# Finer tile pools around attention, and longer assumed landings in the planner, in a hybrid attention and retention block

## The chip, the cores and the metric

The kernel runs on one core of one Trainium2 chip. The metric is the device time of one execution in microseconds (us). The core has TensorE (PE, matmuls; its weight loads are PEld), VectorE (DVE), ScalarE (ACT), GpSimd (POOL) and SyncE (SP), which issues most of the transfers; POOL issues the others. On-chip memory is SBUF; matmuls write into PSUM banks.

## The reference

One layer on x of 1024 positions by 1024 channels, in float32. The input is normalized and projected once; the columns are split over attention (queries, keys and values), retention and gates.

```python
h = rms_norm(x, norm1_g[l])
z = jnp.einsum('bsd,dn->bsn', h, w_in[l])
zq, zkv, zg, zr, zm = jnp.split(z, splits, axis=-1)
y_nsa = nsa_attention(...)   # compressed + selected + sliding-window branches
y_ret = retention(...)       # 4 heads, chunks of 128, group norm, silu gate
u = jnp.einsum('nbsc,ncd->bsnd', jnp.stack([y_nsa, y_ret]), w_branch[l])
gates = jax.nn.sigmoid(zm.reshape(b, s, N_BRANCH, D_MODEL))
mixed = jnp.sum(gates * u, axis=2)
x = x + jnp.einsum('bsd,de->bse', mixed, w_out[l])
h = rms_norm(x, norm2_g[l])
x = x + (jax.nn.silu(h @ ffn_w_gate[l]) * (h @ ffn_w_up[l])) @ ffn_w_down[l]
```

The attention has 8 heads in 2 groups of keys and values. Its first branch attends to 63 compressed keys (a small network over blocks of 32 positions), its second to the 8 blocks of 64 positions that the first one's weights select, its third to the last 512 positions. The feed-forward width is 2816.

## The kernel before, in words

**Arithmetic.** Each float32 operand is split into a high and a low part, and a product is three matmuls (high by high, high by low, low by high). The retention projections use sums of quarters of the normalized input: the tiles gS1 to gS4 hold such sums, the tiles op those of the weights. Each psS, psF, psO, psT names a ring of PSUM banks.

**The order.** The program is not written in the order in which it runs. Each piece of work is a generator that yields operations (`Op`) with a cost, an added latency and the tiles that they read and write. The class `Sched` holds the generators as streams, models the time at which each engine is free and each tile is ready, and always takes the operation with the earliest modelled start; a stream's priority and lateness break near ties. For a transfer it models the issue, the bytes over 360 per ns, and 1000 ns; the `lat` of the operation is added before the tile counts as ready. So a change of an assumed time changes the order on every engine behind it. On the chip, each engine runs its instructions in the order thus written, and a waiting instruction holds those behind it on its engine or queue.

**The tiles.** SBUF is divided in pools that are opened and closed like a stack. A new tile at an address that an earlier, closed pool has covered waits for the last uses of each pool that lies under its own pool. The pools that matter: `gpr` (gS2, gS3 and three buffers gt) on the right side, and `gpl` (gS1, gS4, op, xx, Ta, Tb and three buffers ga) on the left hold the retention projections; both are closed together by `gps.close()`. Behind them `kvp` (kT and vv, keys and values of a group), `ap` (P, pT, comb, cim, cv, cgt and others of the softmax) and `tb` (Mt, Ltri, Fb, which are mask tables; two buffers qt for queries; one buffer zs for gates) are opened on the same addresses.

**The stages,** by the starts in the trace: norm and first projections; the compression (`compress`, L636, run twice, for keys and for values) amid the projections of queries, 60 to 130 us; the retention projections to about 375 us; attention with retention and the gates of the merge as filler, to about 805 us; then `branch1` and `merge_main`, which multiply the two branches by their weights, the output projection and the feed-forward.

**The places that the change and the prediction touch.** In `compress` the gathered input is loaded into the tile cX in two halves, TensorE transposes it 128 columns at a time (L318, psT), VectorE adds the position terms, and TensorE multiplies with cw into psO. The filler beside it is the projection, `whA,H`, and transposes of queries (qcat), whose results SyncE stores to q_scr. `load_group` (L1499) issues kT and vv from POOL, `q_loads` (L827) the qt, also from POOL, and `tables2` builds the mask tables on POOL. The first scores of attention are the matmuls `kc,qt` (compressed keys), then `kT,qt`. The retention projections store their results to r_scr through gt and ga (SP). `merge_gates` multiplies the gates of the merge (`H,wh`), ScalarE writes them to zs, and SP stores them to z_scr. After attention, `y_loads` and `y_split` bring the branch outputs back (yraw) and write them to H. `mx_loads` (L1596) loads what branch1 stored to u_scr, and `merge_out` (L1602) loads the gates again (sgm), combines them with the matmuls' result on VectorE and adds to mx.

The step by which the planner counts a transfer and its latency:

```python
self.bus = max(self.bus, end + 650) + r.bytes / 360.0
end = self.bus + 1000
...
self.ready[k] = max(self.ready.get(k, 0.0), end + r.lat)
```

Of the kernel before, what the change touches and what calls it, by code (L numbers as in the profile page):

```python
# [9 lines left out]
F32 = mybir.dt.float32  # L10
F32R = mybir.dt.float32r
# [5 lines left out]
T = 1024  # L17
# [4 lines left out]
HD = 64  # L22
# [18 lines left out]
def nel(ap):  # L41
    n = 1
    for d in ap.shape[1:]:
        n *= d
    return n
# [212 lines left out]
def kernel(  # L258
# [20 lines left out]
    pe, act, dve, gp, sp = nc.tensor, nc.scalar, nc.vector, nc.gpsimd, nc.sync  # L279
# [26 lines left out]
    def sb_ring(pool, shape, dt, name, bufs):  # L306
        return Ring([lambda: pool.tile(shape, dt, name=name, bufs=bufs)] * bufs)
# [56 lines left out]
    def dma(o, i, eng=None):  # L364
        n = nel(o) * 4 * o.shape[0]
        r = Op("gp", 1040, 0, [o], [i], lambda: gp.dma_start(o, i)) if eng is gp else \  # L366
            Op("sp", 50, 0, [o], [i], lambda: sp.dma_start(o, i))
        r.bytes = n
        return r
# [33 lines left out]
    k_scr = [dram.tile([128, 2, T], F32, name=f"k_scr{br}") for br in range(2)]  # L403
    v_scr = [dram.tile([128, 2, NT, 128], F32, name=f"v_scr{br}") for br in range(2)]
# [50 lines left out]
    rings = {"wo": None}  # L455
# [16 lines left out]
    kT, vv = [[], []], [[], []]  # L472
# [163 lines left out]
    def compress(kv, pc):  # L636
# [8 lines left out]
        for g in range(2):  # L645
            base = c_scr[kv, g]
            yield dma(X[g * 64:(g + 1) * 64, :],
                      bass.AP(tensor=base.tensor, offset=base.offset, ap=[[16 * HD, 64], [1, 2048]]))
# [176 lines left out]
    qt, qref = {}, {}  # L825
# [24 lines left out]
    gps = ExitStack()  # L850
    gpr = gps.enter_context(tc.tile_pool(name="gpr", bufs=1, side="right"))
    gm, gops, gT1, gT2, gT4, gt = {}, {}, {}, {}, {}, {}
    for j in (2, 3):
        gm["S", j] = gpr.tile([128, 2, 4, 512], F32R, name=f"gS{j}")
    gt_ring = Bag([gpr.tile([128, 512], F32, name=f"gt{n}") for n in range(3)])
# [363 lines left out]
    gpl = gps.enter_context(tc.tile_pool(name="gpl", bufs=1))  # L1219
    for j in (1, 4):  # L1220
        gm["S", j] = gpl.tile([128, 2, 4, 512], F32R, name=f"gS{j}")
    gm["Ta"], gm["Tb"] = [sb_ring(gpl, [128, 4, 128], F32, n, 2) for n in ("Ta", "Tb")]
    gm["op"] = [gpl.tile([128, 2, 8, 128], F32R, name="op", bufs=2) for _ in range(2)]
    gt_ring.tiles.extend(gpl.tile([128, 512], F32, name=f"ga{n}") for n in range(3))
    gm["aw"] = gt_ring
    gm["xx"] = gpl.tile([128, 2048], F32, name="xx")
# [5 lines left out]
    es = ExitStack()  # L1232
    kvp = es.enter_context(tc.tile_pool(name="kvp", bufs=1))
    ap_ = es.enter_context(tc.tile_pool(name="ap", bufs=2))
    tb = es.enter_context(tc.tile_pool(name="tb", bufs=1))
    rqs = ExitStack()
    rp = rqs.enter_context(tc.tile_pool(name="rp", bufs=1, side="right"))
    rings["q"] = sb_ring(tb, [128, 2, 4, 128], F32R, "qt", 2)
# [28 lines left out]
    zs_ring = sb_ring(tb, [128, 512], F32, "zs", 1)  # L1267
# [28 lines left out]
    cb_ring = sb_ring(ap_, [128, T], F32, "comb", 1)  # L1296
    comb, pcT, Pt, Ob = {}, {}, {}, {}
# [50 lines left out]
    def select(u, pn):  # L1348
        g, i = u
        yield Wait(lambda: "lt" in fl and "st" in fl)  # L1350
        im = ap_.tile([128, 3, 64], F32, name="cim", bufs=1)
# [4 lines left out]
        v = ap_.tile([128, 4, 16], F32, name="cv", bufs=1)  # L1356
# [7 lines left out]
        gt = ap_.tile([128, 2, 16, 16], F32, name="cgt", bufs=1)  # L1364
# [134 lines left out]
    def load_group(g):  # L1499
        yield Wait(lambda: us[0] in qt)  # L1500
        for br in (1, 0):
            kT[br].append(kvp.tile([128, T], F32R, name=f"kT{br}"))
            vv[br].append(kvp.tile([128, NT, 128], F32R, name=f"vv{br}"))
            yield dma(kT[br][g], k_scr[br][:, g], gp)
            yield dma(vv[br][g], v_scr[br][:, g], gp)
            fl.add("kv1")
        fl.add(("gkv", g))
# [123 lines left out]
    es = ExitStack()  # L1631
# [693 lines left out]
```

## Time and profile before

| | |
|---|---|
| three runs, us | 1597.06, 1598.1, 1599.48 (median 1598.1) |
| profiled execution, us | 1598.91 |
| its span, us | 1597.2 |
| mean granted TensorE clock | 0.993 |
| TensorE busy | 1558.2 us, 98%, 8299 matmuls |
| VectorE busy | 1034.4 us, 65% |
| ScalarE busy | 742.4 us, 46% |
| GpSimd busy | 294.2 us, 18% |

All times of the trace are microseconds from the start of the span. A line of the timeline groups neighbouring instructions of one line and form: start, time that they take together, engine, line, operation, written and read tiles, and a count; in brackets is the idle time of the engine ahead of them, with what ended it. SPq is SyncE's issue of a transfer; its landing is another time, which the view of a tile gives as a minimum, median and maximum. Matmuls are pipelined, so that the last one's end reaches over the next one's start. The granted clock is that of TensorE as a share of full speed.

### The profile page before, as it was taken

The numbers are of one execution on the slowest core, as the hardware profiler recorded it, in microseconds if no ns is written. First come the engines' busy times: TensorE is split into PE (matmuls) and PEld (weight loads), VectorE is DVE, ScalarE is ACT, GpSimd is POOL, SyncE is SP. The second block draws the span as 40 slices with busy tenths as digits, with TensorE's granted clock in tenths as the row PEclk, the third lists the DMA queues.
The fourth block names the chain that finished last, engine by engine and source line by source line (L and its number), as shares of the span: only waits on it lengthen the run. The fifth ranks groups of instructions, "written<-read, shape, count | busy, mean of one in ns | idle before, by whom it ended". The sixth has DMA issues, their size and how long they took to land.

```text
span 1597.2 us, 23177 instructions
## 1 busy us (share of the span) xinstructions
PE 1558.2 (98%) x8299; PEld 1339.0 (84%) x8299; DVE 1034.4 (65%) x2163; ACT 742.4 (46%) x1512; POOL 294.2 (18%) x387
## 2 busy tenths in 40 slices
PE   8989999998999999999999999999999999999999
PEld 8989888887989898897887887888888888788887
DVE  7346655543798967789839449656666555477674
ACT  6234343333777667677524326333333333344442
POOL 4233100002132211221000101332343332000000
PEclk9999999999999999999999999999999999999999
DMA  5565364326333245225476322534344544397521
GB/s 179 159 170 159 111 183 119 118 86 192 99 100 119 81 139 165 73 78 179 140 257 211 132 80 80 184 132 142 135 134 150 178 141 141 120 403 256 180 78 53
DMA packets 191573, 233.06 MB, mean 146 GB/s; under 512 B 21857, under 2 KB 123233, under 8 KB 191202
## 3 DMA queue, kind: packets, MB, share of 16 engines
q1 hardware_dynamic: 178978, 193.84, 37.5%
q0 software_dynamic: 12480, 37.75, 7.1%
q8 instruction: 65, 1.06, 0.3%
q14 instruction: 50, 0.41, 0.1%
HBM read 159.18 MB, written 72.37 MB: 145 GB/s over the span
## 4 chain that ended last, share of the span: by engine, by line
PE 81%; DVE 5%; DMA 3%; ACT 1%; issue 1%; POOL 0%; SPq 0%; DVEq 0%; ACTq 0%
PE psS L313 27%; PE psF L313 26%; PE psO L313 12%; PE psT L313 11%; PE psT L318 4%; DMA qt<-q_scr 1%; DVE P L1302 1%; DMA mx<-u_scr 1%; DVE pT L343 1%; PE psF L318 0%; DVE H L343 0%; DVE wh L343 0%; DMA sg<-z_scr 0%; DVE P L348 0%; DVE T L343 0%
## 5 line engine op out<-in xcount | busy, mean ns | idle before, releaser
L313 PE MATMUL psF<-H,wh 128*128 128x512 f32 x780 | 200.2, 394 | 4.7 <-DVE H L343 2.8
L313 PE MATMUL psS<-H,wh 128*128 128x512 f32 x684 | 187.2, 404 | 3.9 <-DVE sgm L353 3.1
L313 PEld LDWEIGHTS psF<-H,wh 128*128 128x128 f32 x780 | 142.9, 188 | 31.0 <-DVE H L343 3.3
L313 PEld LDWEIGHTS psS<-H,wh 128*128 128x128 f32 x684 | 126.5, 192 | 25.7 <-issue 3.5
L333 ACT ACTIVATE P<-P,pm 128x640 f32<-128x640 f32 (+7 forms) x128 | 94.1, 735 | 45.8 <-DVE pm L1302 43.4
L343 DVE TENSOR_TENSOR pT<-psT,pT 128x512 fp32r<-128x512 f32 (+1 forms) x152 | 92.1, 615 | 32.9 <-ACT pT L333 32.6
L313 PE MATMUL psS<-kT,qt 128*128 128x384 f32 (+3 forms) x384 | 102.9, 346 | 1.0 <-ACT zs L333 0.9
L333 ACT ACTIVATE pT<-psT 128x512 fp32r<-128x512 f32 (+1 forms) x152 | 77.7, 533 | 42.9 <-PE psT L318 42.5
L313 PE MATMUL psO<-pT,vv 128*128 128x256 f32 x528 | 91.3, 290 | 1.8 <-DVE pT L343 1.7
L313 PE MATMUL psS<-whA,H 128*128 128x256 f32 (+1 forms) x672 | 89.9, 288 | 0.0
L313 PEld LDWEIGHTS psO<-pT,vv 128*128 128x128 f32 x528 | 79.2, 189 | 11.2 <-DVE pT L343 4.1
L313 PEld LDWEIGHTS psS<-whA,H 128*128 128x128 f32 x672 | 83.6, 189 | 0.0
L318 PE MATMUL psT<-ident,P 128*128 128x128 f32 x528 | 77.2, 273 | 0.2 <-DVE pT L343 0.2
L313 PEld LDWEIGHTS psS<-kT,qt 128*128 128x128 f32 x384 | 65.7, 192 | 8.1 <-ACT zs L333 1.1
L343 DVE TENSOR_TENSOR wh<-wraw,wh 128x512 fp32r<-128x512 f32 (+1 forms) x55 | 52.3, 959 | 23.1 <-ACT wh L333 23.0
L318 PEld LDWEIGHTS psT<-ident,P 128*128 128x128 f32 x528 | 61.2, 140 | 4.0 <-issue 0.6
L366 POOL DMA_DIRECT2D qt<-q_scr x16 | 12.4, 775 | 280.7 <-DMA r_scr<-gt 189.6
L333 ACT ACTIVATE op<-T 128x512 fp32r<-128x512 f32 x55 | 34.6, 630 | 61.6 <-PE psT L313 34.1
L333 ACT ACTIVATE wh<-wraw 128x512 fp32r<-128x512 f32 (+1 forms) x55 | 44.0, 810 | 32.2 <-PE psT L313 9.9
L343 DVE TENSOR_TENSOR op<-T,op 128x512 fp32r<-128x512 f32 x55 | 48.9, 893 | 15.3 <-ACT op L333 14.4
L313 PE MATMUL psS<-wo,H 128*128 128x512 f32 x216 | 58.6, 393 | 0.0
L313 PE MATMUL psS<-op 128*128 128x512 f32 x234 | 57.6, 389 | 0.0
(505 smaller groups left out, 3556.8 us busy)
## 6 DMA issues: line engine op xcount, KB each, us to landing
wraw<-in_w_in_dram SPq DMA_DIRECT2D x24, 512.0 KB, 4.5
row<-in_ffn_w_down_dram POOLq DMA_DIRECT2D x22, 512.0 KB, 6.0
f_scr<-fs SPq DMA_DIRECT2D x22, 512.0 KB, 2.6
t_scr<-row POOLq DMA_DIRECT2D x22, 512.0 KB, 3.1
qt<-q_scr POOLq DMA_DIRECT2D x16, 512.0 KB, 4.3
st<-t_scr SPq DMA_DIRECT2D x31, 256.0 KB, 5.1
z_scr<-zs SPq DMA_DIRECT2D x24, 256.0 KB, 2.1
wraw<-in_ffn_w_gate_dram SPq DMA_DIRECT2D x12, 512.0 KB, 3.7
```

The costliest lines, as they stand in the source:

```text
L313: lambda: pe.matmul(o, l, r, start=start, stop=stop, skip_group_check=True))
L318: return Op("pe", 109, 100, [o], [i], lambda: pe.transpose(o, i, ident))
L333: return Op("act", c, 150, outs, ins, lambda: act.activation(o, i, func, scale=scale, **kw))
L343: return vop(o, [a, b], lambda: (eng or dve).tensor_tensor(o, a, b, op), eng)
L366: r = Op("gp", 1040, 0, [o], [i], lambda: gp.dma_start(o, i)) if eng is gp else \
L1302: lambda: dve.tensor_tensor_reduce(o, a, b, -sc, init, ALU.add, ALU.min, acc))
```

## The change

Two things are changed. First, `dma` takes a latency: the planner adds 4000 ns to the landing of the two loads of cX, and 3000 ns to those of kT and vv. Second, pools are divided. The buffers gt get a pool of their own (`gtp`), opened ahead of `gpr`. `gpl` becomes `gp1` (gS1), `gp4` (gS4, op, xx, Ta), `gpa` (ga) and `gpb` (Tb). Of `ap`, comb, cim, cv and cgt go to a pool `ap2`. Of `tb`, qt and zs go to a pool `qp`, opened behind it. By their addresses, `kvp` now lies over `gp1` alone, `ap` over `gp4` alone, `ap2` over `gpa` and a part of `gpb`, `tb` over the rest of `gpb` and the start of `gpr`, and `qp` over `gpr` alone (the ends of gS2 and gS3's start). The count of matmuls and of transfers stays; 24 matmuls write a bank of psF in place of one of psS.

```diff
-    def dma(o, i, eng=None):
+    def dma(o, i, eng=None, lat=0):
         n = nel(o) * 4 * o.shape[0]
-        r = Op("gp", 1040, 0, [o], [i], lambda: gp.dma_start(o, i)) if eng is gp else \
-            Op("sp", 50, 0, [o], [i], lambda: sp.dma_start(o, i))
+        r = Op("gp", 1040, lat, [o], [i], lambda: gp.dma_start(o, i)) if eng is gp else \
+            Op("sp", 50, lat, [o], [i], lambda: sp.dma_start(o, i))
...
-                      bass.AP(tensor=base.tensor, offset=base.offset, ap=[[16 * HD, 64], [1, 2048]]))
+                      bass.AP(tensor=base.tensor, offset=base.offset, ap=[[16 * HD, 64], [1, 2048]]), lat=4000)
...
+    gtp = gps.enter_context(tc.tile_pool(name="gtp", bufs=1, side="right"))
+    gt_ring = Bag([gtp.tile([128, 512], F32, name=f"gt{n}") for n in range(3)])
     gpr = gps.enter_context(tc.tile_pool(name="gpr", bufs=1, side="right"))
...
-    gt_ring = Bag([gpr.tile([128, 512], F32, name=f"gt{n}") for n in range(3)])
...
-    gpl = gps.enter_context(tc.tile_pool(name="gpl", bufs=1))
-    for j in (1, 4):
-        gm["S", j] = gpl.tile([128, 2, 4, 512], F32R, name=f"gS{j}")
-    gm["Ta"], gm["Tb"] = [sb_ring(gpl, [128, 4, 128], F32, n, 2) for n in ("Ta", "Tb")]
-    gm["op"] = [gpl.tile([128, 2, 8, 128], F32R, name="op", bufs=2) for _ in range(2)]
-    gt_ring.tiles.extend(gpl.tile([128, 512], F32, name=f"ga{n}") for n in range(3))
+    gp1, gp4, gpa, gpb = [gps.enter_context(tc.tile_pool(name=n, bufs=1)) for n in ("gp1", "gp4", "gpa", "gpb")]
+    gm["S", 1] = gp1.tile([128, 2, 4, 512], F32R, name="gS1")
+    gm["S", 4] = gp4.tile([128, 2, 4, 512], F32R, name="gS4")
+    gm["op"] = [gp4.tile([128, 2, 8, 128], F32R, name="op", bufs=2) for _ in range(2)]
+    gm["xx"] = gp4.tile([128, 2048], F32, name="xx")
+    gm["Ta"] = sb_ring(gp4, [128, 4, 128], F32, "Ta", 2)
+    gt_ring.tiles.extend(gpa.tile([128, 512], F32, name=f"ga{n}") for n in range(3))
     gm["aw"] = gt_ring
-    gm["xx"] = gpl.tile([128, 2048], F32, name="xx")
+    gm["Tb"] = sb_ring(gpb, [128, 4, 128], F32, "Tb", 2)
...
     ap_ = es.enter_context(tc.tile_pool(name="ap", bufs=2))
+    ap2 = es.enter_context(tc.tile_pool(name="ap2", bufs=1))
     tb = es.enter_context(tc.tile_pool(name="tb", bufs=1))
+    qp = es.enter_context(tc.tile_pool(name="qp", bufs=1))
...
-    rings["q"] = sb_ring(tb, [128, 2, 4, 128], F32R, "qt", 2)
+    rings["q"] = sb_ring(qp, [128, 2, 4, 128], F32R, "qt", 2)
...
-    zs_ring = sb_ring(tb, [128, 512], F32, "zs", 1)
+    zs_ring = sb_ring(qp, [128, 512], F32, "zs", 1)
...
-    cb_ring = sb_ring(ap_, [128, T], F32, "comb", 1)
+    cb_ring = sb_ring(ap2, [128, T], F32, "comb", 1)
...
-            yield dma(kT[br][g], k_scr[br][:, g], gp)
-            yield dma(vv[br][g], v_scr[br][:, g], gp)
+            yield dma(kT[br][g], k_scr[br][:, g], gp, 3000)
+            yield dma(vv[br][g], v_scr[br][:, g], gp, 3000)
```

The order of TensorE differs around the compression, at the start of attention, and in the stretch from about 589 to 805 us; elsewhere it is nearly the same. Three places follow.

**TensorE at the first cX** (whA,H is the projection of queries, the filler; cX is the gathered input of the compression). Before:

```order
L313 MATMUL psF<-whA,H 128x256 x13
L317 MATMUL psT<-identr,qcat 128x128 x4
L313 MATMUL psF<-whA,H 128x256 x16
L318 MATMUL psT<-ident,cX 128x128 x4
L313 MATMUL psF<-whA,H 128x256 x14
```

With the change:

```order
L313 MATMUL psF<-whA,H 128x256 x13
L317 MATMUL psT<-identr,qcat 128x128 x4
L313 MATMUL psF<-whA,H 128x256 x35
L313 MATMUL psS<-whA,H 128x256 x18
L318 MATMUL psT<-ident,cX 128x128 x4
L313 MATMUL psS<-whA,H 128x256 x2
```

The transposes of cX stand behind 53 matmuls of the projection, where they stood behind 16. From these transposes to those of the second cX there are 207 matmuls of whA,H, where there were 222, with the same other matmuls and transposes between; on SyncE, the two stores of the query tile q_scr 7 now stand ahead of the second cw, peT and cX, where they stood behind them.

**POOL at the start of attention,** with the semaphores that each transfer waits for (DMAHW are transfers of SyncE's queue). Before:

```order
L366 DMA qt<-q_scr_0_86 128x2x512 [waits DMAHW3_49,DMAHW4_49,DMAHW2_49,DMAHW5_49,DMAHW1_49,DMAHW6_49,DMAHW0_49,DMAHW7_49,DVE_49,Activation_49]
L366 DMA kT_3521<-k_scr_103 128x1024
L366 DMA vv_3522<-v_scr_105 128x1024
L366 DMA qt<-q_scr_1_87 128x2x512
L366 DMA kT_3529<-k_scr_102 128x1024
```

With the change:

```order
L366 DMA qt<-q_scr_0_86 128x2x512 [waits DMAHW4_49,DMAHW5_49,DVE_49,PE_49]
L366 DMA kT_3543<-k_scr_103 128x1024 [waits DMAHW4_49,DMAHW3_49,DMAHW6_49,DMAHW0_49,DVE_49]
L366 DMA vv_3544<-v_scr_105 128x1024 [waits DMAHW7_49,DMAHW4_49,DMAHW1_49]
L366 DMA qt<-q_scr_1_87 128x2x512
L366 DMA kT_3551<-k_scr_102 128x1024 [waits DMAHW5_49]
```

The first qt no longer waits for the last stores of the retention projections; its wait on PE is for the last matmuls that read gS3, a group of twelve on `gS,op` ahead of those on `H,op`. On TensorE, 16 matmuls of `H,wh` now stand between the first scores `kc,qt` and the first `kT,qt`, where there were 3.

**SyncE at the merge** (mx gets the stored result of branch1, sgm the gates). Before:

```order
L367 DMA mx<-u_scr_125 128x512
L367 DMA sgm<-z_scr_0_7967 128x512
L367 DMA mx<-u_scr_126 128x512
L367 DMA sgm<-z_scr_0_7312 128x512
L367 DMA mx<-u_scr_125 128x512
L367 DMA mx<-u_scr_126 128x512
L367 DMA mx<-u_scr_127 128x512
```

With the change:

```order
L367 DMA mx<-u_scr_125 128x512
L367 DMA sgm<-z_scr_0_7938 128x512
L367 DMA mx<-u_scr_126 128x512
L367 DMA sgm<-z_scr_0_7301 128x512
L367 DMA mx<-u_scr_125 128x512
L367 DMA sgm<-z_scr_0_7938 128x512
L367 DMA mx<-u_scr_126 128x512
```

The third sgm stands ahead of the last 13 loads of mx, behind all 16 of which it stood; the fourth stands behind them as before.

More of the change, by code (lines that the diff above doesn't have):

```diff
@@ L1350, in select @@
         yield Wait(lambda: "lt" in fl and "st" in fl)
-        im = ap_.tile([128, 3, 64], F32, name="cim", bufs=1)
+        im = ap2.tile([128, 3, 64], F32, name="cim", bufs=1)
         yield tt(im[:, 0:2], pn[:, 0:2], pn[:, 2:4], ALU.add, gp)
@@ L1355, in select @@
         iv = im[:, 2].rearrange("p (j f) -> p j f", f=4)
-        v = ap_.tile([128, 4, 16], F32, name="cv", bufs=1)
+        v = ap2.tile([128, 4, 16], F32, name="cv", bufs=1)
         yield tt(v[:, 0], iv[:, :, 0], iv[:, :, 1], ALU.add, gp)
@@ L1363, in select @@
         vk = v[:, 2, None, :].to_broadcast([128, 16, 16])
-        gt = ap_.tile([128, 2, 16, 16], F32, name="cgt", bufs=1)
+        gt = ap2.tile([128, 2, 16, 16], F32, name="cgt", bufs=1)
         yield tt(gt[:, 0], vk, vj, ALU.is_equal)
```

## The prediction

> **What bounds the kernel now.** I read the page first: TensorE is busy for nearly the whole span. So only its idle time, and stretches in which its clock is low, can give time back without less work; the change alters no count of matmuls.
>
> ```profile
> span 1597.2 us, 23177 instructions
> PE 1558.2 (98%) x8299; PEld 1339.0 (84%) x8299; DVE 1034.4 (65%) x2163; ACT 742.4 (46%) x1512; POOL 294.2 (18%) x387
> ```
>
> The idle time is 1597.2 − 1558.2 = 39.0 us. Next I read the view of waits of TensorE (what it waited for, us in total, times, longest us):
>
> ```profile
> PE psS L313 <- issue: 4.5, 1, 4.5
> PE psT L318 <- DMA cX<-c_scr: 3.7, 1, 3.7
> PE psT L318 <- issue: 3.6, 1, 3.6
> PE psS L313 <- DVE sgm L353: 3.1, 1, 3.1
> PE psF L313 <- DVE H L343: 2.8, 1, 2.8
> ```
>
> Five single stalls make 17.7 us of the 39.0. "Issue" says that the profile names no releaser; the place in the program tells what was waited for. The timeline of TensorE puts them: the two transposes of cX in the compression, the first scores of attention (kc, qt), the first merged block (sgm), and the first matmul of branch1 (H).
>
> ```profile
> 60.74 2.13 PE L313 MATMUL psF<-whA,H 128*128 128x256 f32 x16
> 66.50 1.09 PE L318 MATMUL psT<-ident,cX 128*128 128x128 f32 x4 [3.62 <-issue]
> ...
> 97.91 5.07 PE L313 MATMUL psS<-whA,H 128*128 128x256 f32 x41
> 102.81 1.47 PE L313 MATMUL psF<-whA,H 128*128 128x256 f32 x11
> 107.93 1.09 PE L318 MATMUL psT<-ident,cX 128*128 128x128 f32 x4 [3.65 <-DMA cX<-c_scr]
> ...
> 360.45 2.88 PE L313 MATMUL psS<-gS,op 128*128 128x512 f32 x12
> ...
> 375.03 1.07 PE L313 MATMUL psS<-H,wh 128*128 128x512 f32 x4
> 380.63 1.89 PE L313 MATMUL psS<-kc,qt 128*128 128x64 f32 x8 [4.54 <-issue]
> ...
> 831.34 5.60 PE L313 MATMUL psT<-H,wh 128*128 128x512 f32 x24
> ```
>
> A stall costs more than its own length. The view by windows of 2 us has the granted clock in the column after POOL (window, length, busy of PE, PEld, DVE, ACT, POOL, clock, DMA share, GB/s):
>
> ```profile
> 66.00:68.00 2.00, 1.50 (x7) 1.53 (x8) 0.92 (x2) 0.07 (x1) 1.27 (x1) 0.50 0.20 76
> 68.00:70.00 2.00, 2.00 (x15) 2.00 (x14) 1.01 (x2) 0.56 (x1) 0.00 (x0) 0.69 0.00 0
> 108.00:110.00 2.00, 2.00 (x11) 2.00 (x12) 0.95 (x2) 0.00 (x1) 0.00 (x0) 0.50 0.03 12
> 110.00:112.00 2.00, 2.00 (x11) 2.00 (x11) 0.34 (x1) 0.59 (x1) 1.28 (x1) 0.50 0.28 109
> 112.00:114.00 2.00, 2.00 (x14) 2.00 (x13) 0.00 (x0) 0.00 (x0) 0.00 (x0) 0.59 0.34 88
> 380.00:382.00 2.00, 1.37 (x7) 1.40 (x7) 0.00 (x0) 0.00 (x0) 1.51 (x25) 0.50 1.07 382
> 382.00:384.00 2.00, 2.00 (x8) 1.71 (x8) 0.67 (x8) 0.77 (x4) 0.00 (x0) 0.50 1.21 409
> 384.00:386.00 2.00, 2.00 (x8) 1.71 (x8) 0.30 (x2) 0.83 (x4) 0.00 (x0) 0.50 1.11 411
> 386.00:388.00 2.00, 2.00 (x10) 1.73 (x11) 1.12 (x8) 1.62 (x8) 0.00 (x0) 0.83 0.13 45
> 840.00:842.00 2.00, 1.95 (x6) 1.60 (x7) 2.00 (x4) 0.16 (x1) 0.00 (x0) 0.67 0.58 227
> 842.00:844.00 2.00, 2.00 (x7) 1.54 (x6) 2.00 (x3) 0.90 (x1) 1.02 (x1) 0.50 0.60 177
> ```
>
> Busy time at half clock does half of its work, so the loss is busy time × (1 − clock). After the first cX it is 1.50 × 0.50 + 2.00 × 0.31 = 1.4 us; after the second (2.00 − the 0.0 idle there) 1.0 + 1.0 + 0.8 = 2.8; at the start of attention 0.7 + 1.0 + 1.0 + 0.3 = 3.0; at the merge 0.65 + 1.0 = 1.7. Together 8.9 us that end with the stalls, if the stalls end.
>
> **The change part by part.** Planner's landing of cX (+4000 ns) and of K and V (+3000 ns) changes no operation, only what the planner believes, and so the order. The pools change no operation either, only which earlier tiles a new tile must wait for.
>
> *First cX.* The order now puts 53 matmuls of whA,H ahead of the transposes instead of 16, so 37 more. One takes 5.07 / 41 = 0.124 us, together 4.6 us. TensorE had come to the transposes at 60.74 + 2.13 = 62.87; now it comes at 67.5. The load is issued from the same place in SyncE's order and so lands by 66.50 as before. I take the whole stall, 3.62, and its clock, 1.4: **5.0 us**. The cover is 1.0 us wide; if the load landed later than 67.5, TensorE would wait again from there.
>
> *Second cX.* From one cX to the next the list has 15 matmuls of whA,H fewer (207 instead of 222): 15 × 0.124 = 1.9 us. The old distance 104.28 − 66.50 = 37.8 less 1.9, less the 1.4 of slow clock, is 34.5, and less small waits about 33.9: TensorE comes at 67.5 + 33.9 = 101.4. The load's place in SyncE's queue changes: two stores of q_scr 7 now stand ahead.
>
> ```profile
> 93.33 2.39 SPq L367 DMA_DIRECT2D cw<-in_cmp_w_dram  x2
> 95.78 2.11 SPq L367 DMA_DIRECT2D peT<-in_cmp_pe_dram  x2
> 97.93 1.89 SPq L367 DMA_DIRECT2D cX<-c_scr  x2
> ...
> DMA to landing us min/median/max: 5.8/7.2/8.6
> ```
>
> The last line is from the view of the tile cX. The load of cw waits for the last reader of the old cw, the matmul cw,ca. In the list this comes after the same 91 matmuls of whA,H behind the first cX as before, with two groups of qcat transposes more; in time it was 19.2 us behind. So it comes near 86.3, and the stores ahead are out by then. From there SyncE issues cw, peT and cX in 2.39 + 2.11 + 1.89 = 6.4 us; the second half of cX goes out at about 92.2 and lands by the median at 99.4, by the maximum at 100.8. Both lie ahead of 101.4. I take 3.65 + 2.8 = **6.5 us**; if the load came as late as before relative to its matmul, nothing.
>
> *Start of attention.* Before, the first qt was held by its pool, which lay over all tiles of the retention projections: POOL's queue waited for the last store of gt.
>
> ```profile
> 373.34 0.94 POOL L366 DMA_DIRECT2D qt<-q_scr  x1 [189.64 <-DMA r_scr<-gt]
> ...
> DMA to landing us min/median/max: 3.8/4.3/9.6
> ```
>
> The second line is from the view of the tile qt. Queued behind that issue on POOL are kT, vv, the second qt and the mask tables; TensorE waits for the qt. Now qt waits for the last matmul that reads gS3, the twelve from 360.45, done at 363.3. It is issued 10.0 us earlier; even after 9.6 us it lands at 373.0, ahead of 375.03 + 1.07 = 376.1, when TensorE comes to it. The kT behind it is covered by 16 matmuls of H,wh (it was 3), 16 × 5.60 / 24 = 3.7 us more. I take 4.54 + 3.0 = **7.6 us**; the least I can read is the stall without the clock.
>
> *Merge.* The third sgm (c=0, first block's second half) now is issued ahead of 13 loads of mx, the fourth still behind all 16.
>
> ```profile
> 824.08 9.65 SPq L367 DMA_DIRECT2D mx<-u_scr  x14
> 834.04 1.68 SPq L367 DMA_DIRECT2D sgm<-z_scr  x3
> ...
> 839.22 1.36 DVE L353 SCALAR_TENSOR_TENSOR sgm<-sgm,psS 128x512 f32<-128x512 f32 x2 [7.05 <-DMA sgm<-z_scr]
> ```
>
> A block's half is 12 matmuls into one bank. TensorE had filled its free banks at 831.34 + 5.60 = 836.94 and waited until VectorE had emptied the bank of the third sgm. With that one early, 12 further matmuls (12 × 0.233 = 2.8 us) run, until 839.7, and then the bank of the fourth is missed. Its load goes out no earlier than before, some 0.55 us after 834.04, so it lands by 839.22 + 0.55 = 839.8 and is through VectorE 0.7 us later. Of 3.11 a stall of about 0.9 is left, 0.2 if it had landed sooner: 2.2 is saved. The stall that is left is well below the 2.82 on H, after which the clock was not lowered:
>
> ```profile
> 736.00:738.00 2.00, 2.00 (x9) 1.66 (x10) 2.00 (x5) 0.21 (x1) 0.00 (x0) 1.00 0.69 206
> ```
>
> So the 1.7 of clock goes too: **3.9 us** (bounds 2.2 and 4.8).
>
> *Gates to branch1.* The first matmul of branch1 waited 2.82 for VectorE's H. Four of these H now stand back to back on VectorE, and TensorE has 14 matmuls and transposes of attention in between, none wider than the 512 columns that take 0.233, so at most 3.3 us; with several of them narrower I take **2.0 us** (0 if VectorE reaches H later, 2.8 if all is covered).
>
> *New small waits.* From 589 to 790 the order of TensorE and VectorE differs in many places. In the windows of 50 us:
>
> ```profile
> 700.00:750.00 50.00, 46.11 (x282) 40.54 (x281) 44.46 (x124) 37.38 (x76) 10.02 (x19) 1.00 0.44 129
> 750.00:800.00 50.00, 49.30 (x291) 43.27 (x290) 42.57 (x97) 30.36 (x54) 2.29 (x1) 1.00 0.48 156
> ```
>
> TensorE idles 3.9 + 0.7 = 4.6 us in these 100, 1.8 beside the stall on H. I allow 2.5 us of new waits, from 0 (below it, −1.8, if those go too) to 8. The first transposes of cPd are in it, which now follow kc,qt after 28 matmuls.
>
> Sum: 5.0 + 6.5 + 7.6 + 3.9 + 2.0 − 2.5 = **22.5 us**. The profiled execution took 1598.91, 0.8 above the median of the three runs, 1598.1; off the median this is **1575.6 us**.
>
> The loss by the clock can be counted in a second way; by the windows it is from 1.4 us (first cX) to 3.0 (attention) for one stall. The Trainium skill, "TensorE: Matmul & The Clock Gate", section "What's actually happening", says that the clock falls to half after an idle window of about 3.4 us and returns after about as long of sustained work. By it each stall loses some 1.7 us of work, an estimate from that page, 6.8 instead of 8.9, and the time would be 2.1 later. The trace agrees in that 2.82 of idling did not lower the clock, and not in the stretch behind 380, which stayed at half for 5.4 us.
>
> **The rivals.**
>
> *Second cX still late.* For it: the load stands behind two more stores and the cover is 0.6 to 2 us thin. Against it: it also starts from an earlier point. Then the 6.5 is not gained: 1582.1.
>
> *Gain of the front is swallowed behind.* VectorE is nearly full while attention and gates run: 87.0 of the 100 us from 700 on, which leaves it 13. If TensorE came early with too little filler, it would wait for softmax. For it: the reordering is in this very stretch. Against: TensorE is idle for only 4.6 of these 100 us now. If it reached the 10 us that are left of VectorE's 13 after the first new waits, the time would be 1585.6.
>
> *A shorter clock loss.* If each low clock has a fixed part of 1.7, as at the merge, and the rest comes from the traffic beside it (DMA share above 1 at 380 to 386), then 2.2 less is gained: 1577.8.
>
> *Nothing.* If landings grew by as much as the planner assumes, or qt were held by something the trace cannot show, time would stay at 1598. Against it: the waits in the order are fewer.
>
> *Slower.* The gates of the merge are the filler for attention. Drawn ahead, they run out, and VectorE sets the pace of the last tiles from 700 on; it decides from the point where TensorE idles more than 22.5 + 3.2 us beyond today's 4.6 in these 100 us, which is all of VectorE's free 13 twice over: 1602 or more.
>
> **How the numbers follow.** Forecast 0.65 (1575.6, its own range 1571 to 1583), second cX late 0.11, swallowed 0.11, shorter clock loss 0.06, nothing 0.03, slower 0.04. All but the last two are faster by over 0.2%, which is 3.2 us and about what a measurement of this kernel can tell from no change: 0.93, with 0.03 for the same and 0.04 slower. The low end takes the whole of all five stalls and clocks, 17.7 + 8.9 = 26.6, with no new wait, 1571.5, and the 1.8 of small waits gone: 1569.7, rounded down. The high end is the swallowed case with the 2.0 of H not gained: 1588.
>
> **What would show it.** In the waits of TensorE neither cX nor kc,qt may stand with more than 1 us, sgm has about 0.9, H below 1. The clock from 66 to 114 and from 376 to 388 is 1.00. POOL issues the first qt some 10 us or more before TensorE uses it. If cX is in the list again, its step was wrong; if the stalls are gone and the time is not, the idle time between 589 and 805 has grown, and the second rival holds. A clock that stays low without a stall would make the sum wrong by up to 8.9.

## The result: 11 us faster, just under half of the forecast

| | runs | median, us | lowest to highest, us | ratio to the kernel before, 95% interval |
|---|---|---|---|---|
| before | 4 | 1597.58 | 1595.42 to 1599.48 | |
| changed | 4 | 1586.61 | 1584.84 to 1589.0 | 0.9933 [0.9914, 0.9952] |
| changed, with the experiments | 6 | 1585.52 | 1582.63 to 1589.0 | 0.9928 [0.9914, 0.9942] |

The kernel is 0.67% faster. The gain is 11.0 us where 22.5 were forecast. The head of the page of the changed kernel:

```profile
span 1585.6 us, 23180 instructions
PE 1550.7 (98%) x8299; PEld 1330.8 (84%) x8299; DVE 1029.3 (65%) x2166; ACT 740.3 (47%) x1509; POOL 295.3 (19%) x387
```

TensorE's idle time is 1585.6 − 1550.7 = 34.9 us; it was 39.0. The busy time fell by 7.5 us: the same 8299 matmuls ran at a mean granted clock of 0.999 instead of 0.993. The view of TensorE's waits shows that four of the five stalls are gone and the one on sgm is shorter (2.4 us in two waits, 3.1 in one before), and what came in their place:

```profile
PE psT L318 <- DVE hx L353: 5.0, 7, 1.5
PE psS L313 <- DVE sgm L353: 2.4, 2, 1.4
PE psO L313 <- DVE cXT L343: 2.3, 2, 1.2
...
PE psT L317 <- DVE qcat L343: 2.2, 1, 2.2
PE psT L317 <- DVE ccat L359: 2.1, 1, 2.1
...
PE psT L317 <- DVE kcat L343: 1.7, 3, 0.8
...
PE psT L317 <- ACT qs L333: 1.0, 1, 1.0
```

Neither cX nor the first kc,qt nor VectorE's H stands in the list. New are cXT, ccat and qs, and the waits on qcat and kcat, 1.0 and 0.4 us before, have grown; all of these are in the compression. Of the 5.0 us on hx (1.9 before), 4.3 lie in the first 35 us of the program, where the order is not changed. The timeline of TensorE puts the others:

```profile
69.69 0.60 PE L318 MATMUL psT<-ident,cX 128*128 128x128 f32 x4
70.05 0.48 PE L313 MATMUL psS<-whA,H 128*128 128x256 f32 x2
72.76 0.51 PE L317 MATMUL psT<-identr,qcat 128*128 128x128 f32 x4 [2.23 <-DVE qcat L343]
...
97.07 0.34 PE L317 MATMUL psT<-identr,ccat 128*128 128x128 f32 x2 [2.10 <-DVE ccat L359]
...
107.75 0.60 PE L318 MATMUL psT<-ident,cX 128*128 128x128 f32 x4
...
375.79 0.97 PE L313 MATMUL psS<-kc,qt 128*128 128x64 f32 x8
...
830.39 5.78 PE L313 MATMUL psS<-H,wh 128*128 128x512 f32 x24 [1.03 <-DVE sgm L353]
...
851.35 11.17 PE L313 MATMUL psS<-wo,H 128*128 128x512 f32 x48 [1.36 <-DVE sgm L353]
```

To see where time went, I cut each trace of TensorE at five starts: the projection's first matmul on psF (58.87 in the kernel before), the first matmul of gS,op (227.17), the first kc,qt (380.63), the last pT,vv (808.17) and the first wo,H (863.51). The rest runs from there to TensorE's last end. All entries are us of one profiled execution each; the experiments in the lower rows follow below.

| kernel | start | compression, to gS | to kc,qt | to last pT,vv | to wo | rest |
|---|---|---|---|---|---|---|
| before | 58.9 | 168.3 | 153.5 | 427.5 | 55.3 | 730.0 |
| changed | 61.5 | 165.5 | 148.8 | 422.7 | 51.1 | 732.3 |
| changed, again | 60.1 | 163.1 | 148.8 | 422.5 | 50.8 | 731.9 |
| cX alone | 59.5 | 166.9 | 153.5 | 426.6 | 55.5 | 730.0 |
| K and V alone | 59.6 | 163.6 | 153.6 | 424.0 | 50.5 | 731.5 |
| pools alone | 63.0 | 164.1 | 148.8 | 424.8 | 56.1 | 730.0 |
| pools, K and V | 59.4 | 164.1 | 148.8 | 420.8 | 51.2 | 731.9 |

The start is 58.9 to 63.0 us among programs whose order is the same up to there, so some 4 us of an execution's time are its own. The compression, where 11.5 us were forecast, gave 2.8 and 5.2 against the first trace, and next to nothing against the three other traces with the old order (163.6 to 164.1). Taken together with the start, which moves the other way in some traces, the compression ends at 223.2 to 227.2 us in the four traces of the table with the old order, and at 223.2 to 227.0 us in the three with the new one.

### The profile page after: what moved, and what is told of

Same layout as the page of the kernel before. It is cut to its first block, busy times and chain, and to the rows that moved or that the text cites. A ratio compares the mean times of both kernels' runs of the same rounds, so it can differ in the third digit from the quotient of the medians.

```text
span 1585.6 us, 23180 instructions
## 1 busy us (share of the span) xinstructions
PE 1550.7 (98%) x8299; PEld 1330.8 (84%) x8299; DVE 1029.3 (65%) x2166; ACT 740.3 (47%) x1509; POOL 295.3 (19%) x387
## 4 chain that ended last, share of the span: by engine, by line
PE 79%; DVE 6%; DMA 3%; ACT 1%; issue 1%; POOL 0%; SPq 0%; DVEq 0%; ACTq 0%; POOLq 0%
PE psF L313 26%; PE psS L313 25%; PE psO L313 12%; PE psT L313 12%; PE psT L318 4%; DMA qt<-q_scr 1%; DVE P L1306 1%; DVE H L343 1%; DVE pT L343 0%; DMA yraw<-y_scr 0%; PE psF L318 0%; DMA sg<-z_scr 0%; DVE sh L343 0%; DMA sgm<-z_scr 0%; DMA rb<-r_scr 0%
## 5 line engine op out<-in xcount | busy, mean ns | idle before, releaser
L313 PE MATMUL psF<-H,wh 128*128 128x512 f32 x804 | 207.4, 395 | 1.9 <-ACT aw L333 1.9
L313 PE MATMUL psS<-H,wh 128*128 128x512 f32 x660 | 177.0, 398 | 2.1 <-DVE sgm L353 1.0
L313 PEld LDWEIGHTS psF<-H,wh 128*128 128x128 f32 x804 | 147.5, 188 | 28.6 <-ACT aw L333 2.7
L313 PEld LDWEIGHTS psS<-H,wh 128*128 128x128 f32 x660 | 120.1, 188 | 23.5 <-DVE sgm L353 1.4
```

The lines of the kernel that those rows point to most:

```text
L313: lambda: pe.matmul(o, l, r, start=start, stop=stop, skip_group_check=True))
```

## First experiments: the three parts apart

The added landing of cX changes the order only in the compression, that of K and V only from the start of attention on, and the pools alone change no order at all but only waits. So the parts can be taken one by one.

**cX alone.** The kernel before, with the argument `lat` of `dma` and

```diff
-                      bass.AP(tensor=base.tensor, offset=base.offset, ap=[[16 * HD, 64], [1, 2048]]))
+                      bass.AP(tensor=base.tensor, offset=base.offset, ap=[[16 * HD, 64], [1, 2048]]), lat=4000)
```

> The kernel before with the planner's 4000 ns on the landing of cX alone; by the written order only the compression's stretch differs from before, and there it is that of the changed kernel. Theory A (filler is only lent: the matmuls drawn ahead of cX are missing beside the chains of the query tiles that follow): both stalls on cX (3.6 and 3.7 us) are gone, new waits on qcat, ccat and cXT of about 8 us stand in the stretch from 60 to 185 us, and the time falls by only some 2.8 us, to about 1595. Theory B (the step holds as predicted and the missing time was lost at the program's start and elsewhere): the time falls by 8 to 11.5 us, to 1586 to 1590.

Measured: 1598.22 us against 1597.62, a ratio of 1.0004 [0.9995, 1.0014] over 12 runs. The part is worth nothing. Its waits on TensorE:

```profile
PE psO L313 <- DVE cXT L343: 2.3, 2, 1.2
PE psT L317 <- DVE ccat L359: 2.2, 1, 2.2
PE psT L317 <- DVE qcat L343: 2.0, 1, 2.0
...
PE psT L317 <- DVE kcat L343: 1.7, 3, 0.9
...
PE psT L317 <- ACT qs L333: 1.0, 1, 1.0
```

They are the same waits as in the changed kernel, 9.2 us in all, where the kernel before has 1.0 on qcat and 0.4 on kcat. Slow clock has not gone from this stretch either; it now follows the wait on qcat, which ends at 70.56:

```profile
71.00:74.41 3.41, 3.41 (x18) 3.41 (x18) 1.30 (x3) 0.60 (x1) 2.42 (x3) 0.50 0.38 120
```

Theory A had the mechanism right and still gave the part too much.

**K and V alone.**

```diff
-            yield dma(kT[br][g], k_scr[br][:, g], gp)
-            yield dma(vv[br][g], v_scr[br][:, g], gp)
+            yield dma(kT[br][g], k_scr[br][:, g], gp, 3000)
+            yield dma(vv[br][g], v_scr[br][:, g], gp, 3000)
```

> The kernel before with 3000 ns on the landing of K and V alone; the order differs from before only from the start of attention to the merge, and there it is that of the changed kernel; the pools are those of before. Theory A (each part is worth what its own stalls are worth): the stall of 4.5 us at the start of attention and its slow clock stay, the stalls on H (2.8) and most of that on sgm (3.1, with 1.7 of clock) go, a new one of 1.4 us at the first wo stands behind: some 4 to 5 us less, about 1593. Theory B (the order of K and V only pays together with the pools): no change, 1597.

Measured: 1589.81 us, ratio 0.9955 [0.9939, 0.9971], 7.8 us by the medians, more than either theory. Two lines of its waits:

```profile
PE psS L313 <- issue: 4.7, 1, 4.7
...
PE psS L313 <- DVE sgm L353: 1.9, 2, 1.3
```

The stall at the first kc,qt stays, as expected of the pools of before. By the table, attention takes 3.5 us less and the piece up to the first wo 4.8 less, and the rest 1.5 more, where a new stall on sgm (0.64, behind the first matmul of wo) and one on hx (0.47) lie: 6.8 us.

**Pools alone.** All pools of the change, without any added landing.

> The kernel before with the divided pools alone, no added landing; the order of all five engines is that of before to the last instruction, only waits differ. Theory A: the first qt is issued some 10 us earlier, the stall of 4.5 us and the slow clock behind it (3.0) go, the stalls on cX, H and sgm stay: about 7.6 us less, 1590. Theory B (with only 3 matmuls of filler between the first kc,qt and the first kT,qt, TensorE then waits for K): 3 to 5 us less, 1593 to 1595.

Measured: 1590.25 us, ratio 0.9951 [0.9938, 0.9964], 7.4 us less: theory A. By the table, 4.7 us come ahead of kc,qt and 2.8 behind it. The first qt is issued 12.3 us before TensorE comes to kc,qt (375.88); POOL waits for the matmuls on gS3 and no longer for a store:

```profile
363.59 0.94 POOL L366 DMA_DIRECT2D qt<-q_scr  x1 [179.97 <-PE psS L313]
```

One more line of this kernel, from its waits, is worth a look, since its order is that of before to the last instruction:

```profile
PE psT L318 <- DMA cX<-c_scr: 1.6, 1, 1.6
```

This is the second cX. It stood with 3.65 us in the trace from which I forecast, and with half clock behind it. In this trace and those of K and V alone and of the next kernel, all in the same order there, it is 1.4 to 1.6 us.

**Pools, K and V together:** the changed kernel without cX.

```diff
-                      bass.AP(tensor=base.tensor, offset=base.offset, ap=[[16 * HD, 64], [1, 2048]]), lat=4000)
+                      bass.AP(tensor=base.tensor, offset=base.offset, ap=[[16 * HD, 64], [1, 2048]]))
```

> The changed kernel without the landing added to cX; so the compression's stretch is in the order of before. Theory A (filler only lent): both stalls on cX are back, the waits on qcat, ccat and cXT are gone, and it is 2 to 4 us slower than the changed kernel, 1588 to 1590. Theory B (the cX part is worth its 11.5 us): 1597 less 12, so 1595 or more is not reached but 1597 less what attention gives, some 1596. If it is no slower than the changed kernel, the cX part is worth nothing at all.

Measured: 1583.09 us, ratio 0.9908 [0.9893, 0.9923], 14.5 us less than before. That is nearly the sum of the two parts (7.8 + 7.4), and not slower than the changed kernel, which has cX besides; both theories failed, and what the expectation said for this case holds, that the part on cX is worth nothing. The intervals of the two ratios (0.9908 [0.9893, 0.9923] here, 0.9928 [0.9914, 0.9942] for the changed kernel in its own later runs) overlap, so that the part on cX costs something is not shown; that it gains nothing is.

## Second experiments: what stands behind the stalls on cX

The wait of 2.23 on qcat ends a chain over four engines. In the changed kernel ScalarE starts it late:

```profile
65.10 0.63 ACT L333 ACTIVATE whA<-rawA 128x512 fp32r<-128x512 f32 x1 [2.90 <-DMA rawA<-in_w_in_dram]
65.63 0.58 ACT L333 ACTIVATE qn<-psS 128x512 f32<-128x512 f32 x1
...
71.26 0.63 ACT L333 ACTIVATE qcat<-qn 128x512 fp32r<-128x512 f32 x1 [4.56 <-POOL qn L343]
```

This is ScalarE's timeline. The first instruction, the split of a weight tile, waits for the load of rawA; the first step of the query tile, qn, stands behind it. VectorE ends the chain:

```profile
71.92 0.69 DVE L343 TENSOR_TENSOR qcat<-qn,qcat 128x512 fp32r<-128x512 f32 x1 [2.04 <-ACT qcat L333]
```

From qn to the end of qcat, 65.63 to 72.61, it takes 7.0 us, and 7.0 in the kernel before too (62.30 to 69.28), where TensorE was late by its own stall on cX and so did not wait. The stall on cX was cover for this chain. To test that, either wait was moved out of the way, with the divided pools, K and V in all of them.

**rawA, on the changed kernel:** the planner adds 3000 ns to its landing, so that it puts qn ahead of the split.

```diff
-        yield dma(raw, w_cols(CH[c], 2 * kk, 2, 256))
+        yield dma(raw, w_cols(CH[c], 2 * kk, 2, 256), lat=3000 if c else 0)
```

> The changed kernel, with 3000 ns more on the landing of rawA in the planner (weights of the query, key and value projection), so that ScalarE's split of rawA no longer stands ahead of the query tile's first step. Theory A (the wait of 2.2 us on qcat comes from ScalarE, which waits in order for rawA): that wait falls below 0.7 us and the stretch up to the last kcat falls by 1.5 to 2.5 us from 123.2, the time to about 1584.5. Theory B (the chain itself is too long for the filler that is left): the wait stays above 1.5 us, 1586.6.

Measured: 1577.2 us, ratio 0.9875 [0.9857, 0.9892]: 19 us below before. ScalarE in this kernel:

```profile
59.35 0.58 ACT L333 ACTIVATE qn<-psS 128x512 f32<-128x512 f32 x1
...
66.21 0.64 ACT L333 ACTIVATE whA<-rawA 128x512 fp32r<-128x512 f32 x1
```

The time is lower than either theory gave. qn now starts 1.0 us after the first cut (58.36), not 4.1 after it (61.49). The wait on qcat is gone, and with it those on cXT and qs, which the expectation had not foreseen; of ccat 0.8 is left:

```profile
PE psT L317 <- DVE ccat L359: 0.8, 1, 0.8
```

The compression takes 159.2 us, 6.3 less than the first trace of the changed kernel. The place where the wait on qcat came from is shown. The order behind it moved as a whole, so which of its steps freed cXT, ccat and qs is not.

**rawA without cX.** The same line, without the added landing of cX.

> The divided pools, K and V at 3000 ns, and 3000 ns on rawA, but nothing on cX; 23 matmuls of filler stand ahead of the first cX. With cX at 0 or 4000 and rawA at 0 or 3000 this is the fourth corner; the stretch from the first psF of the projection to the last kcat took 121.8 (neither), 123.2 (cX alone) and 116.9 us (both). Theory A (each of the two waits covers the other: only with both out of the way is the time gained): a stall on cX of 3 to 4 us is back, the stretch takes 119.5 to 122 us, the time is 1580 to 1583. Theory B (it was ScalarE's order alone): the stretch takes about 117 us, 1577.

Measured: 1589.37 us, ratio 0.9948 [0.9936, 0.996]; slower than without rawA (1583.09, ratio 0.9908 [0.9893, 0.9923]). Two lines of TensorE's timeline:

```profile
66.16 0.63 PE L318 MATMUL psT<-ident,cX 128*128 128x128 f32 x4 [3.94 <-issue]
...
99.91 0.63 PE L318 MATMUL psT<-ident,cX 128*128 128x128 f32 x4 [2.84 <-DMA cX<-c_scr]
```

ScalarE's order alone is not it: the stalls on cX are back and the compression takes 169.7 us. With this the four corners stand, in us of the compression:

| | rawA as before | rawA +3000 ns |
|---|---|---|
| cX as before | 164.1 (pools, K and V) | 169.7 |
| cX +4000 ns | 165.5, 163.1 | 159.2 |

Each edit alone gains nothing or loses; the two together gain 5. That is what two waits do that lie side by side, each the other's cover, and it is theory A by its mechanism. Its numbers for rawA alone were too low: it gave 1580 to 1583 us, and 119.5 to 122 for the stretch to the last kcat, which took 125.7. Mutual cover alone would leave that corner at about 164. Against pools, K and V the kernel has a longer second stall on cX (2.84 for 1.6), a second stretch at half clock behind it, and 3.2 us on kcat for 0.4. Why rawA alone brings these was not tested.

**cX issued early.** The two loads of cX go out ahead of those of cw and peT, with 4000 ns in the planner; rawA is left.

```diff
         X = pc.tile([128, 2048], F32, name="cX", bufs=1)
+        for g in range(2):
+            base = c_scr[kv, g]
+            yield dma(X[g * 64:(g + 1) * 64, :],
+                      bass.AP(tensor=base.tensor, offset=base.offset, ap=[[16 * HD, 64], [1, 2048]]), lat=4000)
         w1 = wpool.tile([128, 16, 128], F32, name="cw1", tag="wh", bufs=2)
...
-        for g in range(2):
-            base = c_scr[kv, g]
-            yield dma(X[g * 64:(g + 1) * 64, :],
-                      bass.AP(tensor=base.tensor, offset=base.offset, ap=[[16 * HD, 64], [1, 2048]]))
```

> The divided pools and 3000 ns for K and V, and both loads of cX issued ahead of cw and peT on SyncE, with 4000 ns of landing in the planner; 38 matmuls of filler stand ahead of the first cX (16 before, 53 in the changed kernel). From the first matmul on psF of the projection to the last transposes of kcat it was 121.3 to 121.8 us in the three runs with the old order, 123.2 and 124.6 in the changed order. Theory A (behind the stalls stand the chains of the query tiles, which ScalarE holds up while it waits for rawA): the stalls on cX are gone, a wait of 1 to 3 us on qcat takes their place, the stretch takes 120 to 122 us, and the time is 1582 to 1584. Theory B (a stall is worth its length and clock, if no filler is borrowed): the stretch takes 115 to 117 us, the time is 1576 to 1578.

Measured: a ratio of 0.989 [0.9871, 0.9909] from four runs of 1577.58 to 1582.23 us (a fifth, of 6478.47, was disturbed and is left out). The compression takes 158.6 us and only 0.3 us of waiting on qcat is left, so theory A failed in its letter; theory B's 115 to 117 us for the stretch to the last kcat came (116.3), though its time did not. The trace shows what else had changed: moving cX moved the load of rawA as well. ScalarE:

```profile
60.01 0.63 ACT L333 ACTIVATE whA<-rawA 128x512 fp32r<-128x512 f32 x1 [2.97 <-DMA rawA<-in_w_in_dram]
...
63.09 0.58 ACT L333 ACTIVATE qn<-psS 128x512 f32<-128x512 f32 x1
```

The split still stands ahead, but it is done before qn could start: qn comes 1.2 us after this kernel's cut (61.92). Again both waits were out of the way, by another way. Theory B's reason, that no filler is borrowed, is not what the gain needs: the kernel with rawA at 3000 ns has 59 matmuls of whA,H between the first psF and the first cX (29 in the old order, 38 here, 66 in the changed kernel) and gains as much, with 159.2.

**Both.** cX early and rawA at 3000 ns.

> Both of these: cX issued ahead of cw and peT, and 3000 ns more on rawA, with the divided pools and K and V. 31 matmuls stand ahead of the first cX. Theory A (the chain behind rawA is what comes next): the stretch takes 118 to 120 us, 2 less than with the early loads alone, time 1580 to 1582. Theory B of the early loads (a stall is worth its length): no difference to the early loads alone.

Measured: 1581.05 us, ratio 0.9894 [0.9878, 0.991], the same as the early loads alone, as theory B said; the compression takes 159.5 us. The second remedy adds nothing to the first, as it must if both do the same for qn.

## Third experiments: the pools and the merge

**No own pool for qt.** All divided pools, without any added landing, but qt and zs again in that of the mask tables.

```diff
-    qp = es.enter_context(tc.tile_pool(name="qp", bufs=1))
...
-    rings["q"] = sb_ring(qp, [128, 2, 4, 128], F32R, "qt", 2)
+    rings["q"] = sb_ring(tb, [128, 2, 4, 128], F32R, "qt", 2)
...
-    zs_ring = sb_ring(qp, [128, 512], F32, "zs", 1)
+    zs_ring = sb_ring(tb, [128, 512], F32, "zs", 1)
```

> Only the divided pools, no added landing, and of them qt and zs put back into the pool of the mask tables (no pool of their own); the order of instructions is that of before. Theory A (the pool of its own for qt is what frees it: else it waits for Tb too, which is in use until the last store of the retention projections is prepared): a stall of 3 to 4.5 us at the first kc,qt is back with its slow clock, and the time is 1594 to 1597. Theory B (the pool of gt alone is enough): the stall is gone, 1590 as with all pools divided.

Measured: 1588.65 us, ratio 0.9945 [0.9925, 0.9965]; the stall is gone as with all pools (0.9951). Theory B: the pool `qp` is not what frees qt.

**A pool for gt alone.** The kernel before, with

```diff
+    gtp = gps.enter_context(tc.tile_pool(name="gtp", bufs=1, side="right"))
+    gt_ring = Bag([gtp.tile([128, 512], F32, name=f"gt{n}") for n in range(3)])
     gpr = gps.enter_context(tc.tile_pool(name="gpr", bufs=1, side="right"))
...
-    gt_ring = Bag([gpr.tile([128, 512], F32, name=f"gt{n}") for n in range(3)])
```

> The kernel before with only the three buffers gt in a pool of their own; gpl, ap and tb are as before, and no landing is added. Theory A (what held qt were the last stores from gt): qt is issued near 367 instead of 373, the stall of 4.5 us at the first kc,qt is gone and the time is 1590 as with all pools divided. Theory B (the pool gpl under ap and tb holds it as well, until the last ga and Tb are free): a stall of 1 to 4.5 us stays, 1592 to 1597.

Measured: 1592.05 us, ratio 0.9967 [0.9954, 0.998], 5.4 of the 7.4 us of all pools. POOL issues qt when the last psF of the projections is done, and TensorE waits for K instead, with slow clock behind (POOL, TensorE, and windows with the clock in the column after POOL):

```profile
365.80 0.94 POOL L366 DMA_DIRECT2D qt<-q_scr  x1 [186.38 <-PE psF L313]
```

```profile
379.82 0.41 PE L313 MATMUL psS<-kT,qt 128*128 128x128 f32 x2 [2.00 <-DMA kT<-k_scr]
```

```profile
380.00:382.00 2.00, 2.00 (x15) 1.88 (x14) 0.60 (x4) 1.29 (x3) 0.00 (x0) 0.80 0.07 25
382.00:384.00 2.00, 2.00 (x12) 2.00 (x11) 1.78 (x3) 2.00 (x6) 0.00 (x0) 0.50 0.00 0
384.00:386.00 2.00, 2.00 (x10) 1.82 (x9) 1.34 (x11) 1.23 (x5) 0.00 (x0) 0.50 0.72 174
```

By time this is at theory B's edge, by place it is neither: the stall at the first kc,qt is gone and another has come. qt is issued 5.9 us ahead of kc,qt (371.67) here and 12.3 us ahead with all pools, so the pool for gt carries most of the gain and the division of `gpl` brings the issue further forward. How much time that part is worth is not shown, since the intervals of the two ratios (0.9967 [0.9954, 0.998] and 0.9951 [0.9938, 0.9964]) overlap.

**The gates of the merge asked for three blocks ahead,** on the fastest kernel (changed, with rawA).

```diff
-            sch.spawn(merge_out(c, half, ring), 1)
+            for m in range(4) if n == 0 else (n + 3,):
+                if m < len(b0_order):
+                    sch.spawn(merge_out(*b0_order[m], f_ring if m < 2 else u_ring), 1)
```

> The changed kernel with 3000 ns on rawA (1577.2 before), and in the merge the gates sgm are asked for three blocks ahead, so that the first four sgm stand behind the first four mx instead of behind all 16; the rest of the order is nearly the same. Theory A (the stall is the issue order on SyncE): the stalls on sgm (1.4 and 0.5) are gone, some 1.5 to 2 us less, 1575 to 1576. Theory B (VectorE is what is late there, it runs 2.0 of 2.0 us in every window around): they stay in another place and the time stays at 1577.

Measured: 1578.2 us, ratio 0.9879 [0.9866, 0.9892], against 0.9875 without. The stalls on sgm are still 2.5 us; they now stand at 0.59 and, behind the first matmul of wo, 1.87:

```profile
842.31 8.04 PE L313 MATMUL psS<-wo,H 128*128 128x512 f32 x34 [1.87 <-DVE sgm L353]
```

Theory A failed; theory B's time and its stall in another place came. Its cause, VectorE being full, is not seen at the first of the two, where VectorE itself waited:

```profile
822.78 0.69 DVE L353 SCALAR_TENSOR_TENSOR sgm<-sgm,psS 128x512 f32<-128x512 f32 x1 [2.79 <-DMA sgm<-z_scr]
```

Ahead of the second, VectorE waited only 0.65 us for sgm in all between 833 and 838 and is busy 2.00 of 2.00 us in each window from 838 to 844, so there theory B's cause is not excluded. What would help was not tried further.

**The changed kernel again,** beside these.

> The changed kernel once more, beside the others on one chip. Theory A (the part on cX costs some 1.5 to 3 us beside the rest): 10.5 to 12 us below the kernel before, and the waits on qcat (2.2), ccat (2.1) and cXT (2.3) are there again in place of the stalls on cX. Theory B (its first profile was an outlier): 14 us or more below, those waits smaller.

Measured: 1585.52 us, 12 us below before, at the edge of theory A's range; that the part on cX costs time is still not shown. In its trace cXT has 2.3 again, qcat 1.5 and ccat 0.5, and the compression takes 163.1 us against 165.5. So the waits on qcat and ccat are 2.3 us shorter here than in the first trace, and the compression is 2.4 shorter; the waits themselves are there in both.

## Where the prediction was right and where it failed

**First and second cX (5.0 + 6.5): wrong, found 0.** This is the step that failed: the prediction took both stalls at their whole length and put what else is due behind them at nothing. The step on the first cX said what covers the load, and that TensorE would wait again from 67.5 if it came later, but not which other waits the same matmuls cover. TensorE came to the first cX 8.2 us after the cut (forecast 67.5 − 58.87 = 8.6) and found it landed, by 0.2 us in this trace and 0.9 in the second one, where 1.0 was forecast. The 37 matmuls drawn forward were filler for the query tile's chain, and that chain was itself late because ScalarE stood at rawA. With cX alone, the waits on qcat, ccat, cXT, qs and kcat are 9.2 us (1.4 before), so 7.8 new us, against some 5.3 that go: 3.7 and 1.6 for the two stalls as the other traces have them. The slow clock behind the first stall only moved behind qcat, and TensorE's idle time in the trace is 39.2 us, where it was 39.0. That the gain was there is shown by the one further edit on rawA, with which the whole change is 19 us better than before.

The other fault is the size of the second stall: 6.5 us were taken from one execution, 3.65 of idling and 2.8 of clock. In the traces of the five programs with the same order there it is 1.4 to 1.8 us. The row was right and not typical.

The forecast of the second load failed too, without a stall to show for it. SyncE was to take up cw near 86.3, with the stores out by then. In the changed kernel:

```profile
86.28 5.92 SPq L367 DMA_DIRECT2D q_scr<-qs  x6
92.66 2.82 SPq L367 DMA_DIRECT2D cw<-in_cmp_w_dram  x2
...
97.31 1.78 SPq L367 DMA_DIRECT2D cX<-c_scr  x2
...
DMA to landing us min/median/max: 6.2/6.7/7.3
```

The last line is from the view of the tile cX from 96 us on. The second half is issued at 98.5 and lands near 105.8, 44.3 us after the cut; the forecast has TensorE there 42.5 us after it (101.4 − 58.87). No stall shows because the waits on qcat and ccat (2.23 + 2.10) held TensorE until 107.75, 46.3 us after the cut. In the second trace of this kernel the load landed 41.9 us after the cut and TensorE came 43.8 after it.

**Start of attention (7.6): right.** Pools alone gave 7.4, 4.7 as the stall and 2.8 as clock (forecast 4.54 and 3.0), and qt was issued at 363.50 where 363.3 was forecast. What it was put down to, qt's own pool, was too wide: a pool for gt is enough for most.

**Merge (3.9): right in place, and a rest behind.** The stall left is 1.03 (forecast 0.9), and the clock stayed up. A stall of 1.36 behind the first matmul of wo came after it, which no step of mine reached. The pieces from the last pT,vv on give 4.2 − 2.3 = 1.9 us in the changed kernel.

**Gates to branch1 (2.0), and new small waits (−2.5): too low.** Together they were to be −0.5. K and V alone brought attention 3.5 us: the stall on H (2.82) and zs (1.2) went and no new waits of that size came.

Of the rivals, a second cX still late left no stall, but its reason, the stores ahead of the load, was there. The one of a gain swallowed behind was right in its kind and wrong in its place: the gain was swallowed before attention, in the compression, by ScalarE and not by VectorE. Its time, 1585.6, is near to the measured one by luck. In attention TensorE's idle time from 700 to 800 fell from 4.6 to 1.0 us, so VectorE did not become the bound there.

## What to carry to other kernels

A stall that ends when one thing arrives covers all that arrives a little earlier: before costing it at its length, list for each engine what is due within that time, and what its queue stands at. A planner's order that hides one load by drawing filler forward takes that filler from the waits behind; the two have to be moved together, and each may look worthless when tried alone. Take the length of a stall from more than one execution where it rests on a transfer, and the slow clock behind it too.

## What the runs showed of the hardware

**Slow clock after a stall depends on when the stall falls.** The first cX had stalls of 3.62 and 3.86 us in the kernel before and in that with divided pools, in the same order. Before, the four transposes behind it ran at half clock at once (1.09 us, the window 66 to 68 at 0.50). With divided pools they took 0.63 us at full clock, and the clock fell 1.2 us after their start (TensorE and windows of the kernel with the pools alone):

```profile
70.81 0.63 PE L318 MATMUL psT<-ident,cX 128*128 128x128 f32 x4 [3.86 <-issue]
```

```profile
70.00:72.00 2.00, 1.19 (x11) 1.22 (x12) 1.21 (x2) 0.00 (x0) 1.20 (x2) 1.00 0.26 98
72.00:74.00 2.00, 2.00 (x12) 2.00 (x11) 0.86 (x2) 0.63 (x1) 0.56 (x1) 0.50 0.00 0
```

And a stall of 2.00 us on K, shorter than the one on H that left the clock alone, was followed by half clock for more than 3 us (rows above). My sentence that a stall well below 2.82 lowers nothing was wrong as a rule; it held at the merge.

The traces show what decides. In each of the 14, every change of the granted clock lies on a grid of steps of 3.41 us, which starts at another time in each execution. From 60 to 1560 us, each of the 19 full-clock steps in which TensorE idled for 1.97 us or more is followed by a step at half clock; after one with 1.81 us or less this never happened. The wait on H is 2.82 us in the kernel before and in the one without a pool for qt. In the first the grid cuts it in two, 1.72 and 1.10 us, and the clock stays (two steps, window, length and TensorE's busy time ahead):

```profile
731.44:734.85 3.41, 1.69 (x9) 1.12 (x8) 3.41 (x6) 3.41 (x8) 1.92 (x2) 1.00 0.47 146
734.85:738.27 3.42, 2.32 (x10) 1.80 (x10) 3.42 (x8) 1.36 (x3) 0.00 (x0) 1.00 0.76 203
```

In the second it falls into one step, and the next one runs at half clock:

```profile
723.33:726.74 3.41, 0.59 (x3) 0.38 (x3) 3.41 (x6) 2.78 (x6) 1.23 (x2) 1.00 0.76 224
726.74:730.15 3.41, 3.41 (x10) 2.63 (x9) 3.41 (x8) 1.44 (x3) 0.00 (x0) 0.50 0.81 230
```

So the row on H from which the prediction took its sentence was luck of the grid. The half clock behind 380 in the kernel before, which the prediction puts at 5.4 us, lasted two steps, from 379.87 to 386.70; that behind the second cX lasted two as well, those behind the first cX and at the merge one. What adds a second step is not shown.

The Trainium skill, "TensorE: Matmul & The Clock Gate", section "What's actually happening", says that the window in which activity is counted runs freely and is not started by the kernel. The runs agree: the grid starts at another time in each trace, and the same stall shows its slow clock in different places. They do not agree with a full window of about 3.4 us of idling as the condition, since 2.00 us of one wait were enough.

**ScalarE waits in order.** The split of rawA held qn for about 3 us though qn's operand was there: in the kernel with rawA at 3000 ns the same qn runs 6.9 us ahead of the split.
